# All three stick-breaking pairs' products in one burst, all three block pairs' in another, and the buffers that this needs

## The chip, the cores and the metric

The kernel runs on one core of a Trainium2 chip, in one launch. The core's engines work side by side from their own instruction lists: PE multiplies matrices, ACT applies functions, DVE does element-wise work and reductions, POOL fills constants, and SP issues the transfers. The metric is the device time in microseconds of one launch; the median of three runs is compared.

## The reference

A decoder trunk of two layers runs over 256 tokens of width 1024 in float32. Each layer is a mixer and then a cross-attention over 256 memory tokens; a root-mean-square norm ends the trunk. The mixer projects the normed tokens once and splits the result among three kinds of heads.

```python
def hybrid_mixer(hn, ...):
    proj = hn @ w_in
    # 6 block-sparse heads of 64: one block of 256 keys, so causal softmax attention
    a_o = moba_attention(a_q, a_k, to_heads(mv, MOBA_HEADS, MOBA_DIM))
    # 4 differential heads: softmax1 - lam * softmax2, then a norm per head
    b_o = diff_attention(b_q, b_k, ...)
    # 6 stick-breaking heads of 64
    c_o = stick_breaking_attention(...)
    merged = concat([a_o * silu(mg), b_o * silu(dg), c_o * silu(sg)])
    return merged @ w_out

def stick_breaking_attention(q, k, v):      # for each block of 128 queries
    z = q @ k.T * scale
    log_beta = log_sigmoid(z)
    log_1m_beta = where(mask, log_beta - z, 0)
    between = reverse_cumsum(log_1m_beta) - log_1m_beta
    w = where(mask, exp(log_beta + between), 0)
    return w @ v
```

## The kernel before

Activations stand transposed, width on the partitions, tokens in the free dimension. For accuracy every large product is made of three: each operand is split into a rounded high half and a remainder (`split`, `load_next`), and high x high, high x low and low x high are added in a PSUM bank. Weights come in granules of 128 x 1024 by DMA into `wraw`; ACT rounds one into `whi` (L150), DVE subtracts it into `wlo` (L151). Six buffers of each hold five granules of lookahead, so a new weight copy waits until PE has finished the granule whose buffer it takes.

PE's instructions stand in the order in which the program is written (a manual schedule around the body). The program interleaves two things by a clock of its own: the main products (`w_stationary`, `t_stationary`, `mixed`, in steps that call `tick`) and small jobs, Python generators that yield how long their PE work takes and how long to wait before they go on. `JOB_SHARE` limits how much of the jobs one tick may bring. ACT and DVE are ordered by the scheduler of the language, which models their times and the buffers; what it decides is fixed in the built program. Tiles come from pools with a number of buffers for each name or tag; a tile may be written only when the buffer it takes is free.

Three kinds of jobs matter. `sb(c, last)` treats a pair of stick-breaking heads: scores in two banks (`stick_banks`), then softplus on ACT and DVE (`softplus`: Abs, Exp, Ln, Exp, three DVE steps, split into hi and lo), then cumulative sums on PE (`stick_weights`: for each head four products at L605 and L606 with hi and lo), an Exp into a pt tile, and last the product of the probabilities with v (`pv`, eight instructions of which two heads share the array's columns). `moba(c)` does softmax numerators for a pair of block heads, three transposes a head (`p_transposed`, L542), a copy into pt (L545) and `pv`. `diff(c)` does the differential heads. `together(pending, last, first, then)` collects the `pv` of several pairs and issues them one after the other when `last` is true; the gate products (L698, L815) follow on DVE.

```python
jobs = [self.job(sb(c, i > 0), SB_START + SB_PACE * i) for i, c in enumerate((1, 2, 0))]
e, y, r, hi, lo = W("sbe"), W("sby"), W("sbr"), W("sbh", R), W("sbl", R)
```

Before, the first two pairs are issued together and the third by itself, in both kinds of jobs. After the blocks' last `pv` come the last output products (`out_part` over range(5, 8)), which begin with chunk 0, the first block pair.

Of the kernel before, what the change touches and what calls it, by code (L numbers as in the profile page):

```python
# [11 lines left out]
F32 = mybir.dt.float32  # L12
R = mybir.dt.float32r
I32 = mybir.dt.int32
AF = mybir.ActivationFunctionType
# [43 lines left out]
SB_WAIT, SB_PACE = 8000, 9000  # L59
# [9 lines left out]
MOBA_START, SB_START, DIFF_START = 14350, 1500, 1000  # L69
# [7 lines left out]
class Trunk:  # L77
# [459 lines left out]
    def p_transposed(self, p):  # L537

        nc = self.nc
        ps = self.bank()  # L540
        for b in range(3):
            nc.tensor.transpose(ps[:, b * 128:b * 128 + 128], p[:, b * 128:b * 128 + 128], self.ident)  # L542
        pt = self.work.tile([128, 512], F32, name="pt", bufs=4)
        with self.urgent():
            nc.scalar.activation(pt[:, 0:384], ps[:, 0:384], AF.Copy)  # L545
        return pt

    def pv(self, v, pts):
# [33 lines left out]
    def softplus(self, ps):  # L582

        nc = self.nc
        z = ps[:, 0:384]
        W = lambda n, dt=F32: self.work.tile([128, 384], dt, name=n)
        e, y, r, hi, lo = W("sbe"), W("sby"), W("sbr"), W("sbh", R), W("sbl", R)
        nc.scalar.activation(e, z, AF.Abs)
        nc.scalar.activation(e, e, AF.Exp, scale=-1.0)
        nc.scalar.activation(y, e, AF.Ln, bias=1.0)  # L590

        nc.scalar.activation(r, y, AF.Exp, scale=-1.0)
        nc.vector.scalar_tensor_tensor(r, e, 1.0, r, OP.add, OP.mult)
        nc.vector.scalar_tensor_tensor(r, r, -1.0, y, OP.add, OP.add)
        nc.vector.scalar_tensor_tensor(e, z, 0.0, r, OP.max, OP.add)
        self.split(e, hi, lo)
        return ps, hi, lo

    def stick_weights(self, ps, hi, lo):

        nc = self.nc
        kw = dict(skip_group_check=True)
        z = ps[:, 0:384]
        for p in (hi, lo):
            nc.tensor.matmul(z, self.trim, p, start=False, stop=False, **kw)  # L605
            nc.tensor.matmul(ps[:, 128:256], self.allm, p[:, 256:384], start=False, stop=p is lo, **kw)  # L606
        w = self.work.tile([128, 512], F32, name="pt", bufs=4)
        with self.urgent():
            nc.scalar.activation(w[:, 0:384], z, AF.Exp)
        return w  # L610


    def mixer(self, l):
# [67 lines left out]
        def together(pending, last, first, then):  # L681

            pending.append((first, then))
            if last:
                outs = [f() for f, _ in pending]
                for o, (_, f) in zip(outs, pending):
                    f(o)
# [3 lines left out]
        def sb(c, last):  # L691
            qk = [x[64 * j:64 * j + 64] for j in range(2) for x in (sqk[c], sqk[3 + c])]
            z = [self.softplus(ps) for ps in self.stick_banks(*qk)]
            yield 1070, SB_WAIT
            w = [self.stick_weights(*x) for x in z]
            yield 1070, PT_WAIT
            together(sbp, last, lambda: self.pv(lambda j, t: sb_v(2 * c + j, t), w),
                     lambda o: nc.vector.tensor_tensor(self.gate[5 + c], o, self.gate[5 + c], OP.mult))  # L698
            yield 720 * len(sbp) * last, 0
            if last:  # L700
                sbp.clear()


        jobs = [self.job(sb(c, i > 0), SB_START + SB_PACE * i) for i, c in enumerate((1, 2, 0))]

        def transposed(x, blocks, dst):
            for j in range(0, len(blocks), 2):
# [87 lines left out]
        def moba(c):  # L795
            self.finish(tj2, tj3)
            if c != 1:

                for i in ((0, 1), (), (2,))[c]:
                    qk = [x[64 * j:64 * j + 64] for j in range(2) for x in (blk(i), blk(3 + i))]  # L800
                    mq[i] = self.score_banks(*qk)
            ps = []
            for b in mq[c]:
                p, r = self.numerators(b, 0.125)
                for t, cc in ((0, slice(0, 128)), (1, slice(128, 384))):
                    nc.vector.tensor_scalar(p[:, cc], p[:, cc], r[:, t:t + 1], None, OP.mult)
                ps.append(p)
            yield (1520, 0, 760)[c], MOBA_WAIT
            pts = []
            for j in range(2):  # L810
                pts.append(self.p_transposed(ps[j]))
                yield 330, (PT_LAST if j else MOBA_NEXT)
            together(mp, c > 0, lambda: self.pv(lambda j, t: tok["t3"][:, t, 64 * (2 * c + j):64 * (2 * c + j) + 64],
                                                pts),
                     lambda o: nc.vector.tensor_tensor(self.gate[c], o, self.gate[c], OP.mult))  # L815
            yield 640 * len(mp) * (c > 0), 0
            if c:
                mp.clear()

        mj = [self.job(moba(c), MOBA_START + MOBA_PACE * c) for c in range(3)]  # L820
# [29 lines left out]
    def cross(self, l):  # L850
# [7 lines left out]
        def head(h, outs):  # L858
            q = self.work.tile([128, 256], F32, name="xq")
            with self.urgent():  # L860
                nc.vector.tensor_tensor(q, outs[h], nr["bc"], OP.mult)
                qh, ql = [self.act.tile([128, 256], R, name=n, tag=f"gate{i + h % 2}")
                          for n, i in (("xqh", 4), ("xql", 6))]
                self.split(q, qh, ql)
            yield 0, Q_WAIT + Q_PACE * h
            ps = self.bank()
            kh, kl = self.xk[h]
            for t in range(2):
                o, c = ps[:, t * 256:t * 256 + 256], slice(t * 128, t * 128 + 128)
                kw = dict(skip_group_check=True)  # L870
                nc.tensor.matmul(o, qh[:, c], kh, start=t == 0, stop=False, **kw)
                nc.tensor.matmul(o, qh[:, c], kl, start=False, stop=False, **kw)
                nc.tensor.matmul(o, ql[:, c], kh, start=False, stop=True, **kw)
            mx = self.work.tile([128, 2], F32, name="mx", bufs=6)
            p = self.work.tile([128, 512], F32, name="prob", bufs=5)
            sm = self.work.tile([128, 2], F32, name="sum", bufs=6)
            with self.urgent():
                nc.vector.tensor_reduce(mx, ps.rearrange("p (t k) -> p t k", t=2), AX.X, OP.max)
                nc.vector.tensor_scalar(mx, mx, -scale, None, OP.mult)
                for t in range(2):  # L880
                    c = slice(t * 256, t * 256 + 256)
                    nc.scalar.activation(p[:, c], ps[:, c], AF.Exp, bias=mx[:, t:t + 1], scale=scale,
                                         accum_out=sm[:, t:t + 1])
                nc.vector.reciprocal(sm, sm)
                for t in range(2):
                    c = slice(t * 256, t * 256 + 256)
                    nc.vector.tensor_scalar(p[:, c], p[:, c], sm[:, t:t + 1], None, OP.mult)
            yield 660, X_WAIT
            pp = self.bank()
            for t in range(2):  # L890
                for k in range(2):
                    nc.tensor.transpose(pp[:, k * 256 + t * 128:k * 256 + t * 128 + 128],
                                        p[:, t * 256 + k * 128:t * 256 + k * 128 + 128], self.ident)
            ph = self.work.tile([128, 512], R, name="pth", tag="pt", bufs=4)
            if h % 2 == 0:
                pl[h // 2] = self.act.tile([128, 2, 512], R, name="ptl", tag=f"t{2 + h // 2}")
            lo = pl[h // 2][:, h % 2, :]
            with self.urgent():
                self.split(pp, ph, lo)
            yield 440, XPT_WAIT  # L900
            while not have_v:
                yield 0, 500
            po = self.bank()
            vh = [self.xv[:, k, h * 128:h * 128 + 128] for k in range(2)]
            vl = [self.xvl[2 * k + h // 2][:, h % 2 * 128:h % 2 * 128 + 128] for k in range(2)]
            for i, (v, p_) in enumerate(((vh, ph), (vl, ph), (vh, lo))):
                for k in range(2):
                    nc.tensor.matmul(po[:, 0:256], v[k], p_[:, k * 256:k * 256 + 256], start=i + k == 0,  # L908
                                     stop=i + k == 3)
            oh[h] = self.act.tile([128, 256], R, name=f"xh{h}")  # L910
            ol[h] = self.act.tile([128, 256], R, name=f"xl{h}")
            with self.urgent():
                self.split(po[:, 0:256], oh[h], ol[h])
            yield 660, 0
# [175 lines left out]
```

## Time and profile before

| what | us |
|---|---|
| median of three runs (404.42 to 404.93) | 404.44 |
| the profiled execution's own time | 403.74 |
| its span, first to last instruction | 401.8 |
| PE busy | 393.0 |
| DVE busy | 315.9 |
| ACT busy | 277.9 |

The span is what the trace covers; 1.94 us of the profiled execution lie outside it. PE's busy time counts overlapping products once. A PE row's duration is longer than its step, since products are pipelined: the time from one start to the next is what a product costs. In a timeline a line may merge several instructions, and then the number behind x says how many.

### The profile page before, as it was taken

The numbers are of one execution on the slowest core, as the hardware profiler recorded it, in microseconds if no ns is written. First come the engines' busy times: TensorE is split into PE (matmuls) and PEld (weight loads), VectorE is DVE, ScalarE is ACT, GpSimd is POOL, SyncE is SP. The second block draws the span as 40 slices with busy tenths as digits, with TensorE's granted clock in tenths as the row PEclk, the third lists the DMA queues.
The fourth block names the chain that finished last, engine by engine and source line by source line (L and its number), as shares of the span: only waits on it lengthen the run. The fifth ranks groups of instructions, "written<-read, shape, count | busy, mean of one in ns | idle before, by whom it ended". The sixth has DMA issues, their size and how long they took to land.

```text
span 401.8 us, 7732 instructions
## 1 busy us (share of the span) xinstructions
PE 393.0 (98%) x2819; PEld 356.7 (89%) x2819; DVE 315.9 (79%) x785; ACT 277.9 (69%) x586; POOL 42.5 (11%) x105
## 2 busy tenths in 40 slices
PE   7999999999999999999999999999999999999994
PEld 6999988877889989988999999888788999998983
DVE  3979969689977968879797865786997696796954
ACT  5879878776956667539385944889776577674843
POOL 4488960000000000000000000000000000000000
PEclk9999999999999999999999999999999999999998
DMA  7986794424354334631737775443246424361002
GB/s 210 348 280 228 237 330 156 156 83 137 134 185 159 104 111 153 213 104 52 240 128 251 228 227 186 142 159 120 78 161 220 153 95 137 107 193 69 1 2 104
DMA packets 19478, 64.10 MB, mean 160 GB/s; under 512 B 2544, under 2 KB 3184, under 8 KB 19440
## 3 DMA queue, kind: packets, MB, share of 16 engines
q1 hardware_dynamic: 19440, 63.61, 46.8%
q8 instruction: 22, 0.36, 0.4%
q14 instruction: 16, 0.13, 0.1%
HBM read 62.55 MB, written 1.05 MB: 158 GB/s over the span
## 4 chain that ended last, share of the span: by engine, by line
PE 93%; DVE 3%; DMA 1%; ACT 1%; SPq 1%; issue 0%
PE bank L383 15%; PE bank L384 14%; PE bank L385 14%; PE bank L401 8%; PE bank L403 7%; PE bank L402 7%; PE bank L973 3%; PE bank L553 2%; PE bank L542 2%; PE bank L908 1%; DMA h<-in_xT_dram 1%; PE bank L470 1%; PE bank L471 1%; PE bank L472 1%; PE bank L605 1%; PE bank L711 1%
## 5 line engine op out<-in xcount | busy, mean ns | idle before, releaser
L151 DVE TENSOR_TENSOR wlo<-wraw,whi 128x1024 fp32r<-128x1024 f32 (+1 forms) x117 | 137.3, 1178 | 39.9 <-ACT whi L150 39.0
L150 ACT ACTIVATE whi<-wraw 128x1024 fp32r<-128x1024 f32 (+1 forms) x117 | 118.4, 1019 | 40.3 <-PE bank L385 21.0
L383 PE MATMUL bank<-xh,whi 128*128 128x256 f32 x416 | 119.8, 288 | 1.4 <-ACT xh L301 1.4
L384 PE MATMUL bank<-xh,wlo 128*128 128x256 f32 x416 | 117.9, 283 | 0.0
L385 PE MATMUL bank<-xl,whi 128*128 128x256 f32 x416 | 117.8, 283 | 0.0
L383 PEld LDWEIGHTS bank<-xh,whi 128*128 128x128 f32 x416 | 79.8, 192 | 3.1 <-ACT xh L301 1.9
L384 PEld LDWEIGHTS bank<-xh,wlo 128*128 128x128 f32 x416 | 79.8, 192 | 0.2 <-DVE wlo L151 0.2
L385 PEld LDWEIGHTS bank<-xl,whi 128*128 128x128 f32 x416 | 79.7, 192 | 0.2 <-DVE xl L302 0.2
L401 PE MATMUL bank<-whi,xh 128*128 128x512 f32 x128 | 52.1, 407 | 0.0
L403 PE MATMUL bank<-whi,xl 128*128 128x512 f32 x128 | 50.1, 392 | 0.0
L402 PE MATMUL bank<-wlo,xh 128*128 128x512 f32 x128 | 50.1, 391 | 0.0
L532 ACT ACTIVATE prob<-prob,mx 128x128 f32<-128x128 f32 (+1 forms) x56 | 24.8, 446 | 10.9 <-DVE mx L529 10.9
L401 PEld LDWEIGHTS bank<-whi,xh 128*128 128x128 f32 x128 | 24.0, 188 | 6.1 <-issue 2.0
L403 PEld LDWEIGHTS bank<-whi,xl 128*128 128x128 f32 x128 | 24.0, 188 | 5.4
L402 PEld LDWEIGHTS bank<-wlo,xh 128*128 128x128 f32 x128 | 24.1, 188 | 4.1
L301 ACT ACTIVATE xh<-h,gains 128x256 fp32r<-128x256 f32 x32 | 14.6, 497 | 8.2 <-DVE h L297 6.3
L383 PE MATMUL bank<-mh,whi 128*128 128x256 f32 x64 | 18.9, 296 | 0.0
L527 DVE CUSTOM_DVE_ANT_0 prob<-bank,cmask 128x128 f32<-128x128 f32 (+1 forms) x56 | 18.0, 351 | 0.3
L385 PE MATMUL bank<-ml,whi 128*128 128x256 f32 x64 | 18.1, 282 | 0.0
L384 PE MATMUL bank<-mh,wlo 128*128 128x256 f32 x64 | 18.1, 282 | 0.0
L312 ACT ACTIVATE sq<-h 128x256 f32<-128x256 f32 x28 | 11.4, 409 | 6.6 <-DVE sqacc L313 6.2
L302 DVE SCALAR_TENSOR_TENSOR xl<-h,gains,xh 128x256 fp32r<-128x256 f32 x32 | 14.4, 481 | 1.7 <-ACT xh L301 1.6
(268 smaller groups left out, 774.1 us busy)
## 6 DMA issues: line engine op xcount, KB each, us to landing
wraw<-in_w_dram SPq DMA_DIRECT2D x107, 512.0 KB, 4.0
wraw<-in_w_dram SPq DMA_DIRECT2D x10, 256.0 KB, 5.1
wraw<-in_memT_dram SPq DMA_DIRECT2D x4, 512.0 KB, 4.9
h<-in_xT_dram SPq DMA_DIRECT2D x3, 256.0 KB, 6.4
out_dram<-wraw SPq DMA_DIRECT2D x2, 288.0 KB, 2.2
wraw<-in_gfin_dram SPq DMA_DIRECT2D x1, 512.0 KB, 5.3
out_dram<-wraw SPq DMA_DIRECT2D x2, 224.0 KB, 2.2
h<-in_xT_dram SPq DMA_DIRECT2D x2, 128.0 KB, 2.9
```

The lines of the kernel that those rows point to most:

```text
L150: nc.scalar.activation(hi[:, c], raw[:, c], AF.Copy)
L151: nc.vector.tensor_tensor(lo[:, c], raw[:, c], hi[:, c].bitcast(F32), OP.subtract)
L301: nc.scalar.activation(h, src[k], AF.Copy, scale=g)
L302: nc.vector.scalar_tensor_tensor(lw, src[k], g, h.bitcast(F32), OP.mult, OP.subtract)
L383: nc.tensor.matmul(outs[m], whi[:, kk, c], xh[k], start=k == 0 and m % 2 == 0, stop=False, **kw)
L384: nc.tensor.matmul(outs[m], wlo[:, kk, c], xh[k], start=False, stop=False, **kw)
L385: nc.tensor.matmul(outs[m], whi[:, kk, c], xl[k], start=False, stop=k == n - 1, **kw)
L401: nc.tensor.matmul(outs[t], xh[k][:, c], whi[:, kk, :], start=first, stop=False)
L402: nc.tensor.matmul(outs[t], xh[k][:, c], wlo[:, kk, :], start=False, stop=False)
L403: nc.tensor.matmul(outs[t], xl[k][:, c], whi[:, kk, :], start=False, stop=last)
L527: nc.vector.tensor_tensor_reduce(s[:, c], ps[:, c], self.cmask[:, c], 1.0, -3.0e38, OP.add, OP.max, accum_out=m[:, t:t + 1])
L532: nc.scalar.activation(s[:, c], s[:, c], AF.Exp, bias=m[:, t:t + 1], scale=scale, accum_out=sm[:, t:t + 1])
```

## The change

`together` gets its last flag only at the third pair: `i > 1` in place of `i > 0` for the stick-breaking pairs, `c > 1` in place of `c > 0` for the blocks. So three pairs' products stand in one burst. For this three pairs of probability tiles must live at once: pt gets six buffers of 384 columns in place of four of 512. The room comes from softplus, where y and lo, which had two buffers each, share three (the tag `sbyl`), and from the cross-attention's pth, which moves to buffers of mT and dT.

```diff
--- before.py
+++ after.py
@@ -540,9 +540,9 @@
         ps = self.bank()
         for b in range(3):
             nc.tensor.transpose(ps[:, b * 128:b * 128 + 128], p[:, b * 128:b * 128 + 128], self.ident)
-        pt = self.work.tile([128, 512], F32, name="pt", bufs=4)
+        pt = self.work.tile([128, 384], F32, name="pt", bufs=6)
         with self.urgent():
-            nc.scalar.activation(pt[:, 0:384], ps[:, 0:384], AF.Copy)
+            nc.scalar.activation(pt, ps[:, 0:384], AF.Copy)
         return pt
 
     def pv(self, v, pts):
@@ -583,8 +583,8 @@
 
         nc = self.nc
         z = ps[:, 0:384]
-        W = lambda n, dt=F32: self.work.tile([128, 384], dt, name=n)
-        e, y, r, hi, lo = W("sbe"), W("sby"), W("sbr"), W("sbh", R), W("sbl", R)
+        W = lambda n, dt=F32, **kw: self.work.tile([128, 384], dt, name=n, **kw)
+        e, y, r, hi, lo = W("sbe"), W("sby", tag="sbyl", bufs=3), W("sbr"), W("sbh", R), W("sbl", R, tag="sbyl", bufs=3)
         nc.scalar.activation(e, z, AF.Abs)
         nc.scalar.activation(e, e, AF.Exp, scale=-1.0)
         nc.scalar.activation(y, e, AF.Ln, bias=1.0)
@@ -604,9 +604,9 @@
         for p in (hi, lo):
             nc.tensor.matmul(z, self.trim, p, start=False, stop=False, **kw)
             nc.tensor.matmul(ps[:, 128:256], self.allm, p[:, 256:384], start=False, stop=p is lo, **kw)
-        w = self.work.tile([128, 512], F32, name="pt", bufs=4)
+        w = self.work.tile([128, 384], F32, name="pt", bufs=6)
         with self.urgent():
-            nc.scalar.activation(w[:, 0:384], z, AF.Exp)
+            nc.scalar.activation(w, z, AF.Exp)
         return w
 
 
@@ -701,7 +701,7 @@
                 sbp.clear()
 
 
-        jobs = [self.job(sb(c, i > 0), SB_START + SB_PACE * i) for i, c in enumerate((1, 2, 0))]
+        jobs = [self.job(sb(c, i > 1), SB_START + SB_PACE * i) for i, c in enumerate((1, 2, 0))]
 
         def transposed(x, blocks, dst):
             for j in range(0, len(blocks), 2):
@@ -810,11 +810,11 @@
             for j in range(2):
                 pts.append(self.p_transposed(ps[j]))
                 yield 330, (PT_LAST if j else MOBA_NEXT)
-            together(mp, c > 0, lambda: self.pv(lambda j, t: tok["t3"][:, t, 64 * (2 * c + j):64 * (2 * c + j) + 64],
+            together(mp, c > 1, lambda: self.pv(lambda j, t: tok["t3"][:, t, 64 * (2 * c + j):64 * (2 * c + j) + 64],
                                                 pts),
                      lambda o: nc.vector.tensor_tensor(self.gate[c], o, self.gate[c], OP.mult))
-            yield 640 * len(mp) * (c > 0), 0
-            if c:
+            yield 640 * len(mp) * (c > 1), 0
+            if c > 1:
                 mp.clear()
 
         mj = [self.job(moba(c), MOBA_START + MOBA_PACE * c) for c in range(3)]
@@ -891,7 +891,7 @@
                 for k in range(2):
                     nc.tensor.transpose(pp[:, k * 256 + t * 128:k * 256 + t * 128 + 128],
                                         p[:, t * 256 + k * 128:t * 256 + k * 128 + 128], self.ident)
-            ph = self.work.tile([128, 512], R, name="pth", tag="pt", bufs=4)
+            ph = self.act.tile([128, 512], R, name="pth", tag=("mT0", "mT1", "mT2", "dT0")[h])
             if h % 2 == 0:
                 pl[h // 2] = self.act.tile([128, 2, 512], R, name="ptl", tag=f"t{2 + h // 2}")
             lo = pl[h // 2][:, h % 2, :]
```

On ACT, in layer 0, this is how the first stick-breaking pair stood before, from the second head's Ln on. Numbers tell buffers apart: 993 to 996 belong to the first head (y, r, hi, lo), 1007 to 1010 to the second; whi is a weight copy, tq a token copy.

```order
L590 ACTIVATE sby_1007<-sbe_1006 128x384
L592 ACTIVATE sbr_994<-sby_993 128x384
L592 ACTIVATE sbr_1008<-sby_1007 128x384
L150 ACTIVATE whi_1039<-wraw_1038 128x1024
L150 ACTIVATE whi_1072<-wraw_1071 128x1024
L329 ACTIVATE rsm_1056<-msm_1055 128x2
L163 ACTIVATE sbh_995<-sbe_992 128x384
L330 ACTIVATE rsm_1056<-rsm_1056 128x2
L163 ACTIVATE sbh_1009<-sbe_1006 128x384
L671 ACTIVATE tq_1137<-bank_964,rsx_529 128x512
L671 ACTIVATE tq_1137<-bank_965,rsx_529 128x512
```

And now, from the first head's split on.

```order
L163 ACTIVATE sbh_995<-sbe_992 128x384
L150 ACTIVATE whi_1072<-wraw_1071 128x1024
L329 ACTIVATE rsm_1056<-msm_1055 128x2
L590 ACTIVATE sby_1007<-sbe_1006 128x384
L330 ACTIVATE rsm_1056<-rsm_1056 128x2
L592 ACTIVATE sbr_1008<-sby_1007 128x384
L671 ACTIVATE tq_1137<-bank_964,rsx_529 128x512
L671 ACTIVATE tq_1137<-bank_965,rsx_529 128x512
L150 ACTIVATE whi_1156<-wraw_1155 128x1024
L609 ACTIVATE pt_1093<-bank_984 128x384
L163 ACTIVATE sbh_1009<-sbe_1006 128x384
```

The second head's Ln and Exp (L590, L592 of 1007 and 1008) now come after the second weight copy, and its split L163 comes after two token copies, a third weight copy and the first head's pt. On PE the trim products L605 and L606 of both heads stand where they stood.

On ACT, around the third pair of layer 0 (1216 to 1220 and 1230 to 1234; t3 is the token copy of the third token group), before:

```order
L590 ACTIVATE sby_1231<-sbe_1230 128x384
L609 ACTIVATE pt_1254<-bank_1101 128x384
L592 ACTIVATE sbr_1218<-sby_1217 128x384
L609 ACTIVATE pt_1260<-bank_1102 128x384
L592 ACTIVATE sbr_1232<-sby_1231 128x384
L713 ACTIVATE dT0_1150<-bank_1262 128x512
L150 ACTIVATE whi_1269<-wraw_1268 128x1024
L163 ACTIVATE sbh_1219<-sbe_1216 128x384
L671 ACTIVATE t3_1304<-bank_1153,rsx_529 128x512
L671 ACTIVATE t3_1304<-bank_1154,rsx_529 128x512
L163 ACTIVATE sbh_1233<-sbe_1230 128x384
```

And now:

```order
L589 ACTIVATE sbe_1230<-sbe_1230 128x384
L713 ACTIVATE dT1_1151<-bank_1280 128x512
L163 ACTIVATE sbh_1219<-sbe_1216 128x384
L671 ACTIVATE t3_1292<-bank_1153,rsx_529 128x512
L590 ACTIVATE sby_1231<-sbe_1230 128x384
L671 ACTIVATE t3_1292<-bank_1154,rsx_529 128x512
L592 ACTIVATE sbr_1232<-sby_1231 128x384
L150 ACTIVATE whi_1298<-wraw_1297 128x1024
L163 ACTIVATE sbh_1233<-sbe_1230 128x384
```

The second head's Ln and Exp (1231, 1232) now stand between and behind the two copies of t3, and its split behind one more weight copy.

On PE, in layer 0, this is the burst of two pairs before (sv and t3 hold v).

```order
L553 MATMUL bank_1280<-pt_1093,sv_961 64x256
L553 MATMUL bank_1280<-pt_1099,sv_961 64x256
L555 MATMUL bank_1280<-pt_1093,sv_961 64x128
L555 MATMUL bank_1280<-pt_1099,sv_961 64x128
L553 MATMUL bank_1285<-pt_1254,sv_961 64x256
L553 MATMUL bank_1285<-pt_1260,sv_961 64x256
L555 MATMUL bank_1285<-pt_1254,sv_961 64x128
L555 MATMUL bank_1285<-pt_1260,sv_961 64x128
```

And the burst of three now, which stands after the third pair's trim products.

```order
L553 MATMUL bank_1387<-pt_1093,sv_961 64x256
L553 MATMUL bank_1387<-pt_1099,sv_961 64x256
L555 MATMUL bank_1387<-pt_1093,sv_961 64x128
L555 MATMUL bank_1387<-pt_1099,sv_961 64x128
L553 MATMUL bank_1392<-pt_1254,sv_961 64x256
L553 MATMUL bank_1392<-pt_1260,sv_961 64x256
L555 MATMUL bank_1392<-pt_1254,sv_961 64x128
L555 MATMUL bank_1392<-pt_1260,sv_961 64x128
L553 MATMUL bank_1397<-pt_1367,t3_1292 64x256
L553 MATMUL bank_1397<-pt_1373,t3_1292 64x256
L555 MATMUL bank_1397<-pt_1367,t3_1292 64x128
L555 MATMUL bank_1397<-pt_1373,t3_1292 64x128
```

The third pair's four products, which stood apart behind six main products, now follow the second pair's. The score products of the first differential half, which stood behind the third pair's trim products, now stand six main products ahead of them.

## Rows read from the trace of the kernel before

**Rows 1.** The page's busy times, and the waits of PE alone (total us, times, longest).
```profile
PE 393.0 (98%) x2819; PEld 356.7 (89%) x2819; DVE 315.9 (79%) x785; ACT 277.9 (69%) x586; POOL 42.5 (11%) x105
...
PE bank L383 <- ACT xh L301: 1.4, 2, 1.2
PE bank L1020 <- DVE warm L1001: 1.2, 1, 1.2
```

**Rows 2.** PE timeline (start us, duration us, engine, line, operation): single and double bursts.
```profile
81.42 0.40 PE L403 MATMUL bank<-whi,xl 128*128 128x512 f32 x1
...
83.53 0.40 PE L402 MATMUL bank<-wlo,xh 128*128 128x512 f32 x1
...
89.86 0.40 PE L403 MATMUL bank<-whi,xl 128*128 128x512 f32 x1
...
91.32 0.39 PE L402 MATMUL bank<-wlo,xh 128*128 128x512 f32 x1
91.55 0.40 PE L403 MATMUL bank<-whi,xl 128*128 128x512 f32 x1
```

**Rows 3.** ACT timeline, layer 0, first stick-breaking pair.
```profile
60.60 0.93 ACT L592 ACTIVATE sbr<-sby 128x384 f32<-128x384 f32 x2
...
64.03 1.06 ACT L150 ACTIVATE whi<-wraw 128x1024 fp32r<-128x1024 f32 x1 [1.54 <-PE bank L403]
...
65.59 0.51 ACT L163 ACTIVATE sbh<-sbe 128x384 fp32r<-128x384 f32 x1
...
66.07 1.38 ACT L671 ACTIVATE tq<-bank,rsx 128x512 f32<-128x512 f32 x2
67.34 1.05 ACT L150 ACTIVATE whi<-wraw 128x1024 fp32r<-128x1024 f32 x1
68.29 0.86 ACT L609 ACTIVATE pt<-bank 128x384 f32<-128x384 f32 x2
```

**Rows 4.** PE timeline, layer 0, first pair's trim products of the second head.
```profile
67.08 0.39 PE L605 MATMUL bank<-sbh,trim 128*128 128x384 f32 x1
...
67.36 0.40 PE L605 MATMUL bank<-sbl,trim 128*128 128x384 f32 x1
```

**Rows 5.** DVE timeline, layer 0: a weight subtraction, and two dependent steps of softplus.
```profile
68.79 1.23 DVE L151 TENSOR_TENSOR wlo<-wraw,whi 128x1024 fp32r<-128x1024 f32 x1
...
80.76 0.56 DVE L593 SCALAR_TENSOR_TENSOR sbr<-sbe,sbr 128x384 f32<-128x384 f32 x1 [2.65 <-ACT sbr L592]
81.35 0.56 DVE L594 SCALAR_TENSOR_TENSOR sbr<-sbr,sby 128x384 f32<-128x384 f32 x1
```

**Rows 6.** Timeline of ACT and of PE, layer 0, second pair.
```profile
74.90 1.05 ACT L150 ACTIVATE whi<-wraw 128x1024 fp32r<-128x1024 f32 x1
...
79.52 0.40 PE L605 MATMUL bank<-sbl,trim 128*128 128x384 f32 x1
```

**Rows 7.** Timeline of PE and of ACT, layer 0, around the third pair.
```profile
83.19 0.50 PE L401 MATMUL bank<-whi,xh 128*128 128x512 f32 x1
...
84.21 1.39 ACT L671 ACTIVATE t<-bank,rsx 128x512 f32<-128x512 f32 x2 [0.81 <-PE bank L403]
...
87.72 0.94 PE L518 MATMUL bank<-dT,dT 32*128 32x128 f32 x16
```

**Rows 8.** Timeline of ACT and of PE, layer 1, first pair.
```profile
260.97 1.05 ACT L150 ACTIVATE whi<-wraw 128x1024 fp32r<-128x1024 f32 x1
...
263.67 0.40 PE L605 MATMUL bank<-sbl,trim 128*128 128x384 f32 x1
```

**Rows 9.** Busy us by stretch (x instructions: PE, PEld, DVE, ACT, POOL), PEclk; opening products.
```profile
396.00:397.00 1.00, 0.00 (x0) 0.00 (x0) 0.55 (x2) 0.69 (x4) 0.00 (x0) 1.00 0.19 70
397.00:398.00 1.00, 0.00 (x0) 0.00 (x0) 0.78 (x4) 0.33 (x2) 0.00 (x0) 1.00 0.00 0
...
399.00:400.00 1.00, 0.00 (x0) 0.00 (x0) 0.00 (x0) 0.00 (x0) 0.00 (x0) 0.50 0.94 354
...
1.24 3.57 PE L1020 MATMUL bank<-warm 128*128 128x256 f32 x15 [1.24 <-DVE warm L1001]
```


## The prediction

> **What bounds the kernel now.** I read the page first: PE is busy for 393.0 of 401.8 us, ACT and DVE are not full [rows 1]. Then the waits of PE alone: two, 2.6 us in all, both in the first 10 us [rows 1]. So everything that PE does in its written order follows without a gap, and a change is worth what it takes from PE's issue time, less what it makes PE wait. PE's order is written out by hand, so PE can do nothing else while one product waits. Third, PE's timeline at single and paired bursts of probability products; fourth, PE, ACT and DVE side by side where the stick-breaking pairs go through softplus, since there ACT's and DVE's rows stand in a new order.
>
> **What the longer bursts save.** A step between two 512-column products is 0.23 us (91.32 to 91.55) [rows 2]. Around a single burst it is 1.46 us from 89.86 to 91.32 where two steps would be 0.46: the burst costs 1.00. Around a double one it is 2.11 from 81.42 to 83.53, so 1.65 [rows 2]. The second pair adds 0.65, and entering and leaving a burst cost 0.35. The change makes one burst of three out of two and one, for the stick-breaking and for the block pairs, in both layers: four entries, 4 x 0.35 = 1.4 us gained.
>
> [...]
>
> **What the buffers cost.** y (L590 to L594) and lo (L164 to L606) had two buffers each and now share three. The buffers go round in the order y, lo, y, lo, and the scheduler answers by placing the second head's Ln only after the first head's lo is under way. In before both heads went through ACT step by step together; now the second head's chain Ln, Exp, L593, L594, L595, L163, L164 starts late, with weight splits between its steps. PE's four trim products of the pair still stand where they stood.
>
> First pair, layer 0. Up to here PE does what it did, so the weight copy that waited for PE until 64.03 [rows 3] waits again until 64.03. It now stands ahead of the second Ln. Ln starts at 65.1, Exp at 65.6, and Exp ends at 66.15 (each takes 0.52, half of 0.93 and a little [rows 3]). ACT then has the token copies (66.07), the next weight copy (67.34) and the first pt (68.29) where it had them [rows 3]; but L163 of the second head, which stood at 65.59 [rows 3], comes behind that pt: 68.29 + 0.37 = 68.66, ending 69.17. PE asks for it at 67.08 [rows 4]: 2.1 us late. On DVE the chain from 66.15 takes 0.59, 0.59 and 0.56 [rows 5] to 67.9, well ahead of that. L164 now stands behind the weight subtraction that ran from 68.79 to 70.02 [rows 5] and can be no earlier this time, so it runs from 70.0 to 70.55; PE asks for it at 67.36 [rows 4]. PE loses 3.2 us, the first wait within the second. Bounds: nothing, if ACT could pass the waiting copy; 1.7 us if only the chain counts and no queue (64.03 + 1.06 + seven steps of 0.51 to 0.59, to 69.0); 3.2 with the queues as written. I take 3.2, as the order is fixed.
>
> Second pair, layer 0 (times of before; all engines follow PE's 3.2 by now). The weight copy at 74.90 [rows 6] stands between Ln and Exp; Exp ends at 76.4, but DVE first does that copy's subtraction to 77.15. L593, L594, L595 to 78.85, L163 to 79.4, L164 to 79.95; PE asks at 79.52 [rows 6]: 0.45 us.
>
> Third pair, layer 0. Call X the start of the third token group's last six products (83.19 in before [rows 7]). The first token copy started 1.02 later (84.21 [rows 7]). PE now has six products (0.34 + 5 x 0.23 = 1.49), six more (1.38), the score quad (0.9, [rows 7]) and six (1.49) before the trim products: they start at X + 5.26 and ask for the second head's lo 0.8 later, X + 6.06. With c the start of the token copy: Ln at c + 0.64, the second copy, Exp from c + 1.69 to 2.2, the weight copy to c + 3.15, L593 and L594 to c + 3.4, the weight subtraction to c + 4.55, L595 to c + 5.1, L163 to c + 5.6, L164 to c + 6.15. With c = X + 1.0 PE waits 1.1 us; but nine ACT instructions of pairs 2 and 3 (4.4 us by these pitches) follow L163 of pair 2, which bring c to X + 1.7: 1.8 us. Bounds 0 (no queues: the bare chain ends at X + 6.1) and 1.8; I take 1.8.
>
> Layer 1. First pair: the trim products stand after the second pair's scores, so there is more room. The copy at 260.97 [rows 8] and the second pair's Abs stand ahead of L163 (262.3), DVE does that copy's subtraction until 263.6, and L164 ends at 264.15 against 263.67 [rows 8]: 0.5. Second pair: by the same steps within 0.1, taken as nothing. Third pair: the same order as in layer 0 and the same distances, 1.8.
>
> Waits together: 3.2 + 0.45 + 1.8 + 0.5 + 1.8 = 7.75 us.
>
> **Parts that cost nothing.** pt in six buffers of 384: the copies already had 384 columns; they no longer wait for a product to free one. The pth tiles go to mT and dT buffers whose last reader ran tens of microseconds earlier. SP and POOL keep their order, so the DMAs do. Scores of the first differential half now stand before the third trim products and their quad later needs four banks beside a three-bank burst; DVE has read the first quad by 92 and PE asks at about 96 (before + 3.7), so there is no wait. The block burst now stands directly before the last products, which begin with its first pair: gate, split and lo (0.42 each) follow the first pair 0.9 us into the burst while two pairs, 1.3 us, still run; lo is ready some 0.1 us before PE asks. If that cover is gone it costs up to 0.5 us a layer, in the range and not in the sum.
>
> **Sum.** Span 401.8 - 1.4 + 7.75 = 408.15; with the 1.94 us around it (403.74 profiled) 410.1. The median of the runs shown, 404.44, is 0.70 above the profiled execution, which gives 410.8.
>
> **Rivals.**
> - The bursts alone count: ACT and DVE deliver the second heads in time. For it speaks that PE never waited here before, against it the written order. It gives 404.44 - 1.4 = 403.0, faster. It is decided in layer 0's first pair: if the second head's L163 runs before 67.1, this is what happens; it stops being faster once PE loses more than 1.4 us in all.
> - Only the first pairs are late; in both third pairs ACT reaches the token copy early and DVE does L595 ahead of the weight subtraction's delay. Then 3.2 + 0.45 + 0.5 - 1.4 = 2.75, so 407.2. For it: the third pair's bound is zero; against it: ACT's row of nine.
> - The gaps also cost PE its clock. [...] The opening 15 products of 256 columns took 3.57 us [rows 9], where 15 steps of half of 0.23 would be 1.7: so about 1.8 us for each fall, and up to three falls: 412.6 to 416.2, mostly 414. [...]
>
> **Numbers.** Forecast 410.8: 0.64; only the first pairs, 407.2: 0.15; clock, 414: 0.12; bursts alone or nearly so: 0.09. The range 406.5 to 414.0 leaves out the last and part of the clock case. About 0.2% (0.8 us) is what a measurement can tell from no change: faster 0.06, same 0.03, slower 0.91.
>
> **What would show it.** Right: PE's list of waits gains L605 on L163 and L164 (sbh, sbl) with about 7 to 8 us, 3 of them at about 67 to 71 us in layer 0's first pair; the second Ln there follows the weight copy at 64.0; burst steps of 2.1 us around three pairs less the first step. Wrong: no PE wait at L605, L163 of the second head ahead of 67 us, or a granted clock under 1.00 in the middle of the trace.

## The result, and the profile after

| | before | after |
|---|---|---|
| median, us (5 runs each) | 404.44 | 414.45 |
| lowest to highest, us | 403.94 to 404.93 | 412.91 to 415.46 |
| profiled execution, us | 403.74 | 414.35 |
| its span, us | 401.8 | 412.3 |
| PE up to the first L345, us | 24.87 | 27.43 |
| from there to the L345 of layer 0's cross-attention, us | 147.72 | 154.12 |
| layer 1, the same stretch, us | 148.81 | 150.31 |

The change made the kernel slower: ratio 1.0242, interval 1.0219 to 1.0265. The forecast was 410.8, its range 406.5 to 414.0; the time is 0.45 us above that range. The last three rows are read from PE's timeline, at the transposes L345 that open each norm's chain. The same two kernels were timed again later: 413.77 against 404.84, 8.9 apart and inside the range. So the range was missed narrowly, and the start, which varies between runs (experiment 8), had a part in it.

The page after, PE's busy time, and the clock granted in 40 slices:

```profile
PE 397.5 (96%) x2819; PEld 359.5 (87%) x2819; DVE 317.4 (77%) x785; ACT 278.4 (68%) x586; POOL 41.3 (10%) x105
...
PEclk9899999899999999999999999999999999999999
```

In the eighth slice (72 to 82 us) and in the second (10 to 21 us) the clock is under 9. PE's waits (total us, times, longest), against the two of [rows 1]:

```profile
PE bank L605 <- ACT sbh L163: 3.5, 3, 2.0
PE bank L383 <- ACT xh L301: 2.4, 3, 1.5
PE bank L1020 <- DVE warm L1001: 1.2, 1, 1.2
PE bank L605 <- DVE sbl L164: 1.2, 2, 0.9
```

L605 now waits, for the two tiles that the prediction named: 4.7 us by this list, where the prediction gave 7 to 8 as its sign. The list counts only idle time; measured from start to start, the steps to L605 are about 6.4 us longer than before. Layer 0's first pair on PE (start, duration, idle time before and what ended it), where the second head's two products stood 0.28 us apart in [rows 4]:

```profile
69.59 0.22 PE L606 MATMUL bank<-sbl,allm 128*128 128x128 f32 x1
71.81 0.44 PE L605 MATMUL bank<-sbh,trim 128*128 128x384 f32 x1 [1.99 <-ACT sbh L163]
72.09 0.22 PE L606 MATMUL bank<-sbh,allm 128*128 128x128 f32 x1
73.18 0.69 PE L605 MATMUL bank<-sbl,trim 128*128 128x384 f32 x1 [0.87 <-DVE sbl L164]
...
73.90 0.58 PE L571 MATMUL bank<-sqk,sqk 64*128 64x128 f32 x1
```

ACT in that stretch, against [rows 3]; the start had already made everything 2.6 us late:

```profile
66.60 1.06 ACT L150 ACTIVATE whi<-wraw 128x1024 fp32r<-128x1024 f32 x1 [0.77 <-PE bank L403]
...
67.66 0.51 ACT L590 ACTIVATE sby<-sbe 128x384 f32<-128x384 f32 x1
...
68.20 0.53 ACT L592 ACTIVATE sbr<-sby 128x384 f32<-128x384 f32 x1
...
69.92 1.05 ACT L150 ACTIVATE whi<-wraw 128x1024 fp32r<-128x1024 f32 x1
70.86 0.48 ACT L609 ACTIVATE pt<-bank 128x384 f32<-128x384 f32 x1
71.23 0.52 ACT L163 ACTIVATE sbh<-sbe 128x384 fp32r<-128x384 f32 x1
```

Take 2.58 off and these are the prediction's steps: the weight copy at 64.02 (64.03 foreseen), Ln at 65.08 (65.1), L163 at 68.65 (68.66). And DVE, where L164 stands behind a weight subtraction [rows 5]:

```profile
71.44 1.22 DVE L151 TENSOR_TENSOR wlo<-wraw,whi 128x1024 fp32r<-128x1024 f32 x1
72.57 0.55 DVE L164 TENSOR_TENSOR sbl<-sbe,sbh 128x384 fp32r<-128x384 f32 x1
```

What the sum lacked comes right behind. Busy time by us (PE, PEld, DVE, ACT, POOL), then the clock, the DMA engines' share and GB/s:

```profile
72.00:73.00 1.00, 0.31 (x2) 0.10 (x1) 1.00 (x2) 0.00 (x0) 0.00 (x0) 1.00 0.00 0
73.00:74.00 1.00, 0.82 (x4) 0.60 (x4) 0.53 (x3) 0.00 (x0) 0.00 (x0) 0.60 0.44 82
74.00:75.00 1.00, 1.00 (x7) 0.91 (x8) 0.00 (x0) 0.49 (x1) 0.00 (x0) 0.50 0.93 340
75.00:76.00 1.00, 1.00 (x7) 0.78 (x4) 0.00 (x0) 0.00 (x0) 0.00 (x0) 0.50 0.32 119
76.00:77.00 1.00, 1.00 (x5) 0.84 (x4) 0.00 (x0) 0.90 (x3) 0.00 (x0) 0.69 0.00 0
```

For some three us after the two gaps (74 to 77 us) PE is full, at a granted clock of 0.50 to 0.69. The score products of the second pair, which take 0.37 at a clock of 1.00 (experiment 3), start with 0.58 above.

The same products of both traces laid side by side by their starts give the account (us): the gaps of layer 0's first pair 3.18, and 1.63 more until the scores and the next steps are through, 4.81 together; second pair 0.57; third pair with its burst 1.32; block pairs -0.31. In layer 1: 0.51, 0.03, 1.36 and -0.31. The stretch ahead of the first changed instruction is 2.58 longer. All of it is 10.5; the parts add up to 0.1 more.

### The profile page after: what moved, and what is told of

Its sections match the earlier page's. It is cut to its first block, busy times and chain, and to the rows that moved or that the text cites. A ratio compares the mean times of both kernels' runs of the same rounds, so it can differ in the third digit from the quotient of the medians.

```text
span 412.3 us, 7728 instructions
## 1 busy us (share of the span) xinstructions
PE 397.5 (96%) x2819; PEld 359.5 (87%) x2819; DVE 317.4 (77%) x785; ACT 278.4 (68%) x586; POOL 41.3 (10%) x105
## 4 chain that ended last, share of the span: by engine, by line
PE 84%; DVE 8%; ACT 4%; DMA 2%; issue 1%; SPq 1%; DVEq 0%; ACTq 0%
PE bank L383 14%; PE bank L385 14%; PE bank L384 14%; PE bank L401 6%; PE bank L403 6%; PE bank L402 5%; PE bank L973 3%; DVE wlo L151 2%; PE bank L553 2%; DMA h<-in_xT_dram 2%; PE bank L542 2%; PE bank L908 1%; PE bank L470 1%; PE bank L472 1%; PE bank L471 1%; ACT whi L150 1%
## 5 line engine op out<-in xcount | busy, mean ns | idle before, releaser
L532 ACT ACTIVATE prob<-prob,mx 128x128 f32<-128x128 f32 (+1 forms) x56 | 24.8, 445 | 10.9 <-DVE mx L529 10.7
```

The source lines that it names most:

```text
L532: nc.scalar.activation(s[:, c], s[:, c], AF.Exp, bias=m[:, t:t + 1], scale=scale, accum_out=sm[:, t:t + 1])
```

## The experiments

Each ran on the chip beside the kernel before. The medians of before in the three batches were 404.84, 404.45 and 404.83. For traces I give "own part": from the first L345 to the end of the span. It is 376.94 and 377.29 in two profiles of before, 384.86 and 385.13 in two of after. "Entries" are the stretches of small products that stand between long ones in PE's order: 80 in before. The number depends on what one calls long; the differences between kernels do not.

**1. The buffers alone.** Before, with this line changed (and `W` passing the tag on):
```diff
-        e, y, r, hi, lo = W("sbe"), W("sby"), W("sbr"), W("sbh", R), W("sbl", R)
+        e, y, r, hi, lo = W("sbe"), W("sby", tag="sbyl", bufs=3), W("sbr"), W("sbh", R), W("sbl", R, tag="sbyl", bufs=3)
```


> The kernel before with one edit: y and lo of softplus share three buffers; the bursts and the probability buffers stay as before. If the shared buffers cost the time (my theory), PE waits at L605 for the second heads' sbh and sbl as after the change did (2.0 and 0.9 us at layer 0's first pair), the granted clock falls behind these gaps there, and the time is that after the change plus the burst entries that are not saved (measured 0.31 to 0.35 each, four of them): 414.45 + 1.3 = 415.8. If instead the joined bursts and what they move cost the time (rival), this kernel stays at the 404.4 of before. If only the start's loss of 2.6 us is the chance of one run, it is about 413.

Measured 415.06 (ratio 1.026, 1.0235 to 1.0286): the shared buffers alone cost all of it. Its waits of PE:

```profile
PE bank L605 <- ACT sbh L163: 3.0, 3, 2.0
PE bank L605 <- DVE sbl L164: 2.8, 4, 0.9
```

In this profile the clock falls twice in layer 0, behind the first and behind the third pair's gaps:

```profile
73.00:74.00 1.00, 1.00 (x4) 0.81 (x3) 0.00 (x0) 1.00 (x4) 0.00 (x0) 0.50 0.09 29
...
97.00:98.00 1.00, 1.00 (x4) 0.81 (x3) 1.00 (x9) 0.82 (x4) 0.00 (x0) 0.50 0.06 16
```

**2. The bursts alone.** After, with the removed line above put back, and `ctmp` in a buffer of `sqk5` to make room.

> The kernel after the change with one edit: y and lo have two buffers each again, as before (the room comes from a 1 KB constant that moves into a buffer used later). The joined bursts and the six smaller buffers stay. My theory: no wait at L605, and four entries less than before at 0.31 to 0.35: 404.44 - 1.3 = 403.1. The rival, that the joined bursts cost the time: about 414. If the clock at the start falls in every layout of this family, 405.7.

Measured 405.29 (1.0013, 0.9995 to 1.0031): no wait at L605, so the buffers are the cause; but the saving isn't there either. In its trace the burst itself waits: PE's step at the third pair, and on ACT the third pair's two copies of probabilities (L609), with another softmax's steps (L532) between them:

```profile
92.72 1.14 PE L553 MATMUL bank<-pt,t 128*64 128x256 f32 x3
...
93.70 0.38 PE L553 MATMUL bank<-pt,t 128*64 128x256 f32 x1
...
94.23 0.50 PE L401 MATMUL bank<-whi,xh 128*128 128x512 f32 x1
```
```profile
91.66 0.47 ACT L609 ACTIVATE pt<-bank 128x384 f32<-128x384 f32 x1
...
92.91 0.47 ACT L609 ACTIVATE pt<-bank 128x384 f32<-128x384 f32 x1
```

The first three of L553 take 1.14 where the others take 0.60 for four. From the third pair's first product to the next main product 1.51 pass (92.72 to 94.23); in after, whose burst does not wait, it is 0.75 (100.86 to 101.61). Each layer loses some 0.76 by it.

**3. The waits filled.** After, with, in the second head of layer 0's first pair alone:
```diff
         for p in (hi, lo):
+            for i in range((16, 7)[p is lo] if fill else 0): nc.tensor.matmul(*dummy, start=True, stop=True)
             nc.tensor.matmul(z, self.trim, p, start=False, stop=False, **kw)
```
`fill` is true for that head only; `dummy` is 256 columns of a bank that nobody reads and two views of `warm`, which holds zeros.

> The kernel after the change, with products of zeros into a bank that nobody reads, put before the second head's two trim products of layer 0's first pair: 16 and 7 of 128x256, some 1.9 and 0.8 us, where PE waited 1.99 and 0.87. The waits stay, but PE works through them. If the granted clock falls there because PE stands still (theory), it stays at full speed in 73 to 77 us and the time is 1.2 us shorter than after the change: 413.2. If the clock falls for another reason, or the products make the two trims late, it stays at 414.4 or above.

Measured 411.14; after, run again in the same batch, 413.77. The trims come no earlier, but PE works on (in this kernel L605 is the filling, L606 the trim), and the clock stays at 1.00:

```profile
69.13 2.12 PE L605 MATMUL bank<-warm 128*128 128x256 f32 x16
71.28 0.44 PE L606 MATMUL bank<-sbh,trim 128*128 128x384 f32 x1
...
71.62 1.05 PE L605 MATMUL bank<-warm 128*128 128x256 f32 x7
72.66 0.44 PE L606 MATMUL bank<-sbl,trim 128*128 128x384 f32 x1
...
73.08 0.37 PE L571 MATMUL bank<-sqk,sqk 64*128 64x128 f32 x1
```
```profile
72.00:73.00 1.00, 1.00 (x8) 0.77 (x6) 1.00 (x4) 0.00 (x0) 0.00 (x0) 1.00 0.00 0
73.00:74.00 1.00, 1.00 (x11) 0.77 (x9) 0.01 (x1) 0.49 (x1) 0.00 (x0) 1.00 0.84 225
74.00:75.00 1.00, 1.00 (x8) 0.87 (x7) 0.00 (x0) 0.64 (x2) 0.00 (x0) 1.00 0.76 299
```

Layer 0 takes 152.58, 1.54 less than after's 154.12, with the same waits in place: that is the clock's price in this trace. The medians differ by more, 2.6 us.

**4. After again.** Unaltered.

> The kernel after the change, unaltered, for its start: in the profile of after, PE was 2.6 us late before the first changed instruction, with the third and fourth input transfers late and the clock at 0.6 in 12 to 16 us. If that was the chance of one run, PE reaches the first transposes (L345) at about 24.9 us here as before, and the time is about 412. If it belongs to the kernel, 27.4 us again and 414.4.

Measured 413.77 (1.0224, 1.0195 to 1.0253); L345 at 26.96, so the start was late here too, and this run does not settle whose it is. Layer 0 took 154.10, with the clock at 0.50 in 74 to 77 us again.

**5. The rotation.** After, with softplus given both banks of a pair:
```diff
+        for ps in banks:      # y of one head, y of the other
+            ... the four steps on ACT (L588 to L592)
+        for i, (ps, e, y, r, hi) in enumerate(todo):      # lo, lo
+            ... L593 to L595, then lo = W("sbl", R, tag="sbyl", bufs=3) and the split
```


> The kernel after the change with the same three shared buffers, but softplus written in two stages (both heads' four ACT steps, then both heads' DVE steps), so that the buffers go round in the order y, y, lo, lo. My theory is that the order of the rotation and not the number of buffers makes the second head late: no wait above 0.3 us at L605, and a time like the kernel with buffers of their own (405.3), 8 to 9 us below after. If three buffers are simply too few, PE still waits at L605 and the time stays within 2 us of 414.

Measured 404.36 (0.9998, 0.9982 to 1.0014). The same three buffers, no wait at L605: it is the order y, lo, y, lo in which they went round, not their number. The old way of writing softplus, with buffers of its own, did not wait either (experiment 2).

**6. The burst later.** f_rotation, with `PT_WAIT + 650 * last` ahead of the stick-breaking burst.

> f_rotation, with the stick-breaking burst one step of six products later (the planner's wait of the last pair 650 ns longer). In the kernel with own buffers the joined burst waited in its middle 0.65 us (0.21 + 0.29 + 0.15 above the usual steps) in both layers for the third pair's second probabilities. If that wait took what the joined burst saves, this kernel is 1.0 to 1.3 us below f_rotation (two waits of 0.65, some of it covered by a burst that starts sooner), about 404.2, and its profile shows no wait in the burst. If the saving never existed, it equals f_rotation.

Measured 404.98 (1.0001, 0.9982 to 1.0019); expectation wrong. The wait inside the burst is gone, but the second score quad behind it now waits, in both layers, until DVE has read the burst's banks; own part 377.75 against 376.80 in f_rotation:

```profile
97.94 0.92 PE L518 MATMUL bank<-dT,dT 32*128 32x128 f32 x10 [0.17 <-DVE gate L698]
```

**7. The block pairs' burst alone.** f_rotation, with `sb(c, i > 0)` as before.

> f_rotation with the stick-breaking pairs in bursts of two and one as before; only the block pairs go in one burst. Expected: two entries saved at 0.31 to 0.44, so 0.6 to 0.9 us below before, 404.1. If the block burst also waits inside for its last probabilities, no change from before.

Measured 404.87 (0.9997, 0.998 to 1.0013): too small for the timing. Own part 376.39, 0.55 and 0.90 below the two profiles of before, with 78 entries.

**8. Before again.** Unaltered.

> The kernel before, unaltered, for its start. In six profiles PE reached the first transposes (L345) at 24.87 (before) to 27.43 us (after), with the same instructions up to there. If the start is a matter of chance, it differs from 24.87 by some tenths or more here; if before always starts early and after always late, 24.9 again.

One run, 404.9. L345 at 25.67, 0.8 later than in the first profile of before. In the fourteen profiles it lies between 24.87 and 27.43; in experiment 9, whose instructions up to there are those of after, at 25.24. It belongs to the run, not to the change: the 17 runs of before in the first batch fall apart as well, eleven at 403.8 to 405.2 with a mean granted clock of 0.993 to 0.998 and six at 405.9 to 406.4 with 0.991 to 0.993; f_rotation's late profile, 405.56, had 0.992. In the six profiles at 26.9 or later the clock also fell between 10 and 21 us, in the eight at 26.2 or earlier it did not: without the three profiles in which it fell behind the gaps at L605 too, the mean granted clock was 0.992 to 0.993 in the late ones and 0.995 to 0.999 in the early ones. Just before, PE waits for the first token tiles (xh). In the six it stood still there for 1.55 to 2.25 us at a time. So in f_rotation (26.97):

```profile
10.70 0.39 PE L383 MATMUL bank<-xh,whi 128*128 128x256 f32 x1 [2.06 <-ACT xh L301]
...
13.00:14.00 1.00, 1.00 (x6) 1.00 (x6) 1.00 (x4) 1.00 (x4) 0.00 (x0) 0.50 1.01 347
```

and in this run of before:

```profile
10.79 0.39 PE L383 MATMUL bank<-xh,whi 128*128 128x256 f32 x1 [1.72 <-ACT xh L301]
...
13.00:14.00 1.00, 1.00 (x11) 1.00 (x10) 1.00 (x3) 1.00 (x3) 0.00 (x0) 1.00 1.03 361
```

In the other seven no such wait was over 1.27. The waits for the input go with the fall, but this run's 1.72 did not bring one and 1.55 in after's first profile did; what decides it in a run stays open.

**9. One pair mended.** After, with the softplus of experiment 5 for `c == 1 and l == 0` alone.

> The kernel after the change, with softplus in two stages (rotation y, y, lo, lo) in one place alone: the first stick-breaking pair of layer 0. PE's order stays that of after, ACT's and DVE's differ there alone. The two timings of after are 414.45 and 413.77, mean 414.1. By my prediction that pair's waits are worth 3.2 us: 410.9. With the clock that falls behind them, as aligned in the trace of after (4.81 us), 409.3; if in other runs it falls for longer than in the profiled one, below 409. If the clock's fall has another cause than these waits, it stays at about 410.9 and the clock still falls near 73 us.

Measured 408.18 (1.0088, 1.0067 to 1.0108), 5.6 to 6.3 below the two timings of after. Its layer 0 takes 149.31, 4.81 less than after's, as aligned, at a clock of 1.00. The 0.8 to 1.5 that the medians differ by beyond that is not explained by this run; part of it can be the start, which was early in its profile (25.24) and late in both of after.

**10 to 12. Both joined bursts, and the entries really saved.** f_rotation with, in this order, the third pair earlier (m1), the scores later (m2), or both (m3):
```diff
-        jobs = [self.job(sb(c, i > 1), SB_START + SB_PACE * i) for i, c in enumerate((1, 2, 0))]
+        jobs = [self.job(sb(c, i > 1), SB_START + SB_PACE * i - 700 * (i == 2)) for i, c in enumerate((1, 2, 0))]
-MOBA_START, SB_START, DIFF_START = 14350, 1500, 1000
+MOBA_START, SB_START, DIFF_START = 14350, 1500, 2000
```


> f_rotation with the third stick-breaking pair starting 700 ns of the planner's time earlier. PE then has its trim products and the first score quad in one stretch again as before, so both joined bursts really save an entry: 76 stretches of small products between the long ones, where before had 80 and f_rotation and j_moba_only 78. j_moba_only's own part (its span from the first L345 on) was 0.55 us below before for two entries fewer. So 1.1 us below before here, some 403.4 against 404.5; the burst may wait inside as in f_rotation (0.37 each), then 0.4 and 404.1. If the entries are not what counts, no change from f_rotation (404.4).

> f_rotation with the differential scores 1000 ns of the planner's time later instead: also 76 stretches, trim products and first scores together, but the third pair where f_rotation had it. Expected as m1_pair_earlier: 403.4, or 404.1 if the burst waits inside. If the later scores make the differential chain late, 404.5 or more.

> f_rotation with the third pair 700 ns earlier and the scores 1000 ns later, so that 18 instead of 12 long products stand between the joined burst and the second score quad, which needs the banks that the burst holds until DVE has read them. Expected 403.4; if the second quad waited for those banks in m1 or m2, it does not here, and this is the fastest of the three by what it waited.

| | median, us | ratio to before (404.83) | own part, us | entries |
|---|---|---|---|---|
| m1 | 403.56 | 0.9970 (0.9954 to 0.9986) | 375.97 | 76 |
| m2 | 405.53 | 1.0022 (1.0005 to 1.0039) | 377.49 | 76 |
| m3 | 403.26 | 0.9961 (0.9948 to 0.9975) | 376.07 | 76 |

m1 and m3 beat both kernels, by 0.3 to 0.4% against before. What they gained is seen on PE. In f_rotation the scores (L518) and the third pair's trims stood apart, and the scores took 1.17,

```profile
87.04 1.17 PE L518 MATMUL bank<-dT,dT 32*128 32x128 f32 x16
...
89.63 0.34 PE L605 MATMUL bank<-sbh,trim 128*128 128x384 f32 x1
...
92.26 0.65 PE L553 MATMUL bank<-pt,sv 128*64 128x256 f32 x4
```

and in m3 they follow each other, 86.40 being the last trim, and the scores take 0.94:

```profile
86.40 0.22 PE L606 MATMUL bank<-sbl,allm 128*128 128x128 f32 x1
86.55 0.94 PE L518 MATMUL bank<-dT,dT 32*128 32x128 f32 x16
...
89.01 0.65 PE L553 MATMUL bank<-pt,sv 128*64 128x256 f32 x4
```

Measure these stretches as the prediction measured its bursts, from the last long product before to the second one behind, with two long steps, 0.46, in each number. Trims and scores together take 2.62 in before; where nothing waits, scores alone take 1.53 and trims alone 1.61. So parting them costs only 0.06. The rest is waits: f_rotation's scores take 1.75, 0.22 more than they need, and its joined burst 3.03, where m3's takes 2.76. Per layer m1 and m3 win some 0.5 over f_rotation by these three, and most of it is the waits, not the entry.

m2 missed: not the differential chain but the third pair itself was late, in both layers:

```profile
88.40 0.45 PE L605 MATMUL bank<-sbl,trim 128*128 128x384 f32 x1 [0.69 <-DVE sbl L164]
```

m1's second quad did not wait, so the reason given for m3 had nothing to act on; the two own parts differ by 0.1.

## Why the prediction was right and wrong

**Right: the place and the mechanism.** The second heads come late because y and lo share buffers in the order y, lo, y, lo (experiments 1, 2 and 5). The weight copy, Ln and L163 came within 0.02 us of the times foreseen. Layer 0's first pair was to cost PE 3.2 and its gaps are 3.18. The second pair was 0.45 and is 0.57; layer 1's first 0.5 and is 0.51; its second nothing and is 0.03.

**Wrong: the clock was left out of the sum.** The step that failed is the rival "the gaps also cost PE its clock": I gave it 0.12 and put nothing for it into the sum, and it came true. Against it stood that the clock at the kernel's end was still 1.00 from 396 to 398 us, with PE at rest [rows 9], and that the longest gap I reckoned with was 1.7. The gap is 1.99, then 0.50 of work (71.81 to 72.31), then 0.87, and the clock fell to 0.50 in both profiles of after. The price for a fall was about right (1.8; 1.54 measured by filling the gaps), but as an estimate only: it came from the 3.57 us of the opening products, and the trace of before has the clock at 1.00 from 1 to 5 us, so no run shows that a fall made them slow. That the rival's 414 met the time is luck: by its own count 414 is two falls, and behind the waits there was one (412.6); the late start can make up the rest. With the gaps filled the kernel's own part is 383.30, 6.0 to 6.4 above the two profiles of before, and the sum without a clock had 6.35. Full of products of zeros, the stretch kept 1.00 (71 to 76 us in experiment 3). How much rest it takes for the clock to fall the traces don't settle: experiment 1's third pairs had two steps of 0.78 and 1.04 us on PE in layer 0 and of 0.71 and 1.04 in layer 1 (0.06 is usual), and the clock fell only in layer 0.

**Right in size, but not alone: the term of -1.4.** I counted four entries saved at 0.35. In after the joined stick-breaking burst takes 2.10 from its start to the next main product (99.51 to 101.61; 2.1 foreseen). Measured as 1.46 and 2.11 were, it takes 2.76 (99.19 to 101.95), so 0.35 is saved in each layer; the block pairs save 0.31 each. What I put at nothing is what came with it. The first scores now stand ahead of the third pair's trims, six long products apart. The parting itself costs 0.06. But the scores come too early: by the trace their fourth product starts at 93.28, right behind the end of the second token copy at 93.24. That takes some 0.37 in each layer (1.90 where scores alone take 1.53) and eats what the burst saves. As measured, the joined burst leaves out one switch from the main products' 128*128 to 128*64 and one back, and saves 0.31 to 0.35; the trims run in 128*128 like the main products on either side, and parting them from the scores costs 0.06. What in such a switch takes the time is not shown.

**Wrong the other way: the third pairs.** They were to wait 1.8 in each layer; the steps at L605 are 0.89 and 0.25 longer, 1.14. In layer 0 the token copy starts 1.6 after the six products (1.7 foreseen):

```profile
91.57 0.67 ACT L671 ACTIVATE t<-bank,rsx 128x512 f32<-128x512 f32 x1
...
92.56 0.68 ACT L671 ACTIVATE t<-bank,rsx 128x512 f32<-128x512 f32 x1
```
```profile
89.96 0.48 PE L401 MATMUL bank<-whi,xh 128*128 128x512 f32 x1
...
92.89 1.31 PE L518 MATMUL bank<-dT,dT 32*128 32x128 f32 x16
...
97.05 0.45 PE L605 MATMUL bank<-sbh,trim 128*128 128x384 f32 x1 [0.73 <-ACT sbh L163]
```

The first fence is ACT's, the second PE's. The chain behind the copy came as foreseen, within 0.2; but the score quad took 1.31, where 0.94 stood in [rows 7], so PE asked 0.4 later. Part of the 1.8 moved into the quad. In all the stretch costs 1.32, and I had 1.8 - 0.35 = 1.45: the waits at L605 were too long in the sum and the quad's 0.37 was missing, two errors that met.

**Not foreseen: the start.** 2.6 of the 10.5 us between the two profiles lie ahead of the change. By experiment 8 they are the runs' and no effect of it: in the first batch after's profile was a late one, and before's highest time, 404.93, looks like none, so the 10.0 between these medians holds some of it. Own part against own part, the change costs 7.6 to 8.2 us; the sum had 6.35, and the clock is most of what lacks.

**The rivals.** "Bursts alone" is false for this kernel, and its 403.0 is about what m1 and m3 reach, once the rotation and the planner's times are mended: 403.56 and 403.26, 1.3 and 1.6 below before, where 1.4 was the term. "Only the first pairs" is false: the third pairs wait too (97.05 above), and experiment 9, with layer 0's first pair mended, still loses 0.9%.

## What to carry to other kernels

When tiles of two steps of one chain share rotating buffers, look at the order in which they go round before their number: y, lo, y, lo serialises two heads, y, y, lo, lo does not, with the same memory. Where PE follows a written order, price a wait at its length, and see whether the clock falls behind it: here gaps of 2.0 and 0.9 us cost 3.18 and, by the work at 0.50 behind them, 1.54 more. And look at the order as built, not at the diff: joining two bursts moved other products ahead, where what they read or write was not ready, and two waits of 0.2 to 0.4 us ate a saving of 0.35.

## What the runs showed of the hardware

The clock fell to 0.50 behind 2.0 and 0.9 us of rest with 0.50 us of work between, in work that was otherwise full (after, 74 to 76 us); 23 products of zeros in these gaps kept it at 1.00 and made layer 0 1.54 us shorter (2.6 between the medians), though nobody reads what they compute. It fell at the start in some runs and not in others of the same instructions, behind waits of 1.55 to 2.25 us, with L345 between 24.87 and 27.43 us. One switch fewer from the main products (128*128) to products of two heads side by side (128*64) and back saved 0.31 to 0.35 us in after, 0.35 in the stick-breaking and 0.31 in the block burst.
